# Two-layer hybrid block in fp32: normed feed-forward features made earlier, their low parts on GpSimd, paired up passes from tile 4

## The chip, the cores and the metric

The kernel runs on one core of a Trainium2 chip. The core has five engines that work side by side, each through its own queue in order: TensorE (PE, matrix products), VectorE (DVE), ScalarE (ACT), GpSimd (POOL) and SyncE (SP, which issues most of the DMAs). They wait for each other through semaphores. SBUF holds the tiles; TensorE writes its products to PSUM, which has eight banks of 128 partitions by 2 KB. The metric is the device time of one execution in microseconds, as a median over runs.

## The reference, cut to what matters

Two layers over 256 tokens of width 1024. Each layer has three branches (a gated spatial mixer, a state-space mixer, a differential attention) that are merged and projected, and then the feed forward with which the change deals:

```
x = x + merged @ w_out[layer]
h = rmsnorm(x, ffn_norm_g[layer])                        # x * rsqrt(mean(x*x) + EPS) * g
up = causal_dwconv(h @ ffn_w_up[layer], ffn_conv_w[layer], ffn_conv_b[layer])   # 3 taps along the tokens
gate, val = jnp.split(up, 2, axis=-1)                    # 2816 features each
x = x + (jax.nn.silu(gate) * val) @ ffn_w_down[layer]
```

All data are fp32.

## The kernel before, in words

**Products in two parts.** TensorE's operands are split in two: a high part (rounded to the format of the product) and a low part (what is left). A product of fp32 accuracy is then three products: high by high, high by low and low by high (`mm3`, lines 278 to 280). Weights arrive by DMA in one stream of blocks `raw` (1 MB, two halves each). For each half ScalarE makes the high part `whi` (line 231) and VectorE the low part `wlo` (line 235), both 128x1024. There are five buffers of each (`NWB`), and the program makes them four halves ahead of their use, so a new `whi` waits until TensorE is done with the half that had its buffer. The numbers in `whi49_0` are the block and its half.

**The feed forward.** The hidden features are worked through in 22 tiles j of 128 gate and 128 value features. Of each tile, "up" makes gate (m = 0) and value (m = 1) from one half of weights each. After tile 3, and then after each second tile, comes a "down" block that adds two finished tiles to the four accumulators `acc`. The order on TensorE is up 0, 1, 2, 3, down 0, up 4, 5, down 1, up 6, 7, down 2 and so on.

The up products come in two forms:

- Tiles before `MERGE` use features that are scaled by the norm's weight but not yet divided by the norm (`f_hi`, `f_lo`), since the norm of a token isn't known while they run. Each half is 24 products of 256 columns (`feat_half`). The result is multiplied by the norm's row (`fn_row`, one factor for each token) when it is taken out of PSUM, by `normed` (line 712, VectorE, tile `fu`).
- Tiles from `MERGE` on use features `hm` that are fully normed, with high and low parts beside each other. One product of 512 columns gives high by high and high by low, one of 256 columns gives low by high: 16 products a half (`feat_merged`, lines 299 to 303). Each half then takes a bank of its own, and `gather` adds its two parts: a copy on ScalarE (line 1095) and an addition on VectorE (line 1096).

**Making `hm`.** The generator `renorm` makes `hm` in four blocks b of two feature tiles each. In the kernel before: VectorE multiplies x by the norm's row (line 1072, tile `xn`, 128x512), ScalarE scales each half of it by the weight column `gcol` (line 1077, 128x256), ScalarE rounds it to the high part (line 1078), and VectorE subtracts to get the low part (line 1080). It runs as a side job: `tick` is called after each up or down half block and advances the job by its rate (0.5 here, so one step every two halves), and `finish` forces what is left before tile `MERGE`. The job starts after tile 1, once the norm's row is there.

**From tile to `act`.** For each tile, `hidden` runs the three-tap convolution on `fu`: for each m one ScalarE operation (line 756) and two VectorE operations on the tile `fy` (line 761, 128x255 and 128x254). For each second tile follow, on both tiles at once, silu on ScalarE (line 1117, the first one with a table load ahead of it), the product of gate and value on VectorE (line 1118, `fy<-fy`), and the split in `act`: high part on ScalarE (line 347), low part on VectorE (line 349). Down 0 uses the `act` of tiles 0 and 1.

**The order on the engines.** The program is written once for all engines, and a scheduler of the framework sets the order in each engine's queue from the order of writing, from priorities and from its own estimates. The queues are then fixed; on the chip each engine goes through its queue in order. Tiles of kinds `s2` (`fu`, `xn`, seven buffers) and `s4` (`hm`, `fy`, `act`, nineteen) share their slots, and a new tile waits until the last reader of its slot is done.

Of the kernel before, what the change touches and what calls it, by code (L numbers as in the profile page):

```python
# [14 lines left out]
AF = mybir.ActivationFunctionType  # L15
ALU = mybir.AluOpType
# [4 lines left out]
P = 128  # L21
D = 1024
S = 256
# [11 lines left out]
HP = 200  # L35


LAG, MERGE = 3, 7
CUM_WAIT = 6
ROW_WAIT = 2  # L40
WARM = 11
# [68 lines left out]
def ffn_order():  # L110
    order = []
    done = 0
    for j in range(NFT):
        order.append(("up", j))
        if j >= LAG and j % 2 == 1 and j < NFT - 1:
            order.append(("down", done))
            done += 1
    while done < NFT // 2:
        order.append(("down", done))
        done += 1  # L120
    return order
# [8 lines left out]
def block_kernel(ctx: ExitStack, tc: tile.TileContext, x, wstream, wdt, rows, prol, pcols, gains, gmw, consts, out):  # L130
    nc = tc.nc
# [9 lines left out]
    def ps(name):  # L141
        return pspool.tile([P, 512], F32, tag="ps", name=name)

    def s4(name, shape, dt=F32):
        return big.tile(shape, dt, tag="s4", name=name, bufs=NS4)

    def s2(name, shape, dt=F32):
        return sm.tile(shape, dt, tag="s2", name=name, bufs=NS2)
# [3 lines left out]
    x_sb = cpool.tile([P, 8, S], F32, name="x_sb")  # L152
    gcol = cpool.tile([P, L * G_N], F32, name="gcol")
# [86 lines left out]
    def next_half():  # L240

        while len(ready) <= AHEAD and stream["i"] < n_halves:
            load_half()
        return ready.popleft()
# [10 lines left out]
    def add_side(gen, rate):  # L255
        side.append([gen, rate, 0.0])
        return side[-1]
# [14 lines left out]
    def finish(e):  # L272
        while e in side:
            step(e)
# [31 lines left out]
    def feat_pair(o, h_hi, h_lo):  # L306

        halves = [next_half() for _ in range(2)]
        for k0, k1 in ((0, 6), (6, 8)):
            for m, (whi, wlo) in enumerate(halves):  # L310
                for k in range(k0, k1):
                    ks = slice(k * P, (k + 1) * P)
                    mm3(
                        o[:, m * S : (m + 1) * S], whi[:, ks], wlo[:, ks], h_hi[:, k, :], h_lo[:, k, :],
                        k + m == 0, k + m == 8,
                    )
        tick()
        tick()
# [130 lines left out]
    for l in range(L):  # L449
# [589 lines left out]
        for kh in range(2):  # L1039
            for t2 in range(4):  # L1040
                whi, wlo = next_half()
                for m in range(2):
                    t = 2 * t2 + m
# [18 lines left out]
        nff = {}  # L1062
        nf_side = add_side(norm_factors(f"fn{l}", nff, 2, 1), 1)

        def renorm():

            t = {}
            for b in range(5):
                if b < 4:
                    hm.append(s4(f"hm{l}_{b}", [P, 2, 2, S], F32R))  # L1070
                    t[b] = s2(f"xn{l}_{b}", [P, 2, S])
                    nc.vector.tensor_tensor(
                        t[b], x_sb[:, 2 * b : 2 * b + 2, :], nff["row"].unsqueeze(1).to_broadcast([P, 2, S]), op=ALU.mult
                    )
                    for m in range(2):
                        g = l * G_N + 8 + 2 * b + m
                        nc.scalar.activation(t[b][:, m, :], t[b][:, m, :], AF.Identity, scale=gcol[:, g : g + 1])
                    nc.scalar.activation(hm[b][:, :, 0, :], t[b], AF.Copy)
                if b:
                    nc.vector.tensor_tensor(  # L1080
                        hm[b - 1][:, :, 1, :], t[b - 1], hm[b - 1][:, :, 0, :].bitcast(F32), op=ALU.subtract
                    )
                yield
# [89 lines left out]
        for kind, j in ffn_order():  # L1173
            if kind == "down" and not acc:
                acc.extend(ps(f"acc{l}_{b}") for b in range(4))
            if kind == "up":
                if j == MERGE:
                    finish(hm_side)
                if j < MERGE:
                    outs[j] = [ps(f"up{l}_{j}")]  # L1180
                    if j == 0:
                        feat_pair(outs[j][0], f_hi, f_lo)
                for m in range(2):
                    if j >= MERGE:
                        outs.setdefault(j, []).append(ps(f"up{l}_{j}_{m}"))
                        feat_merged(outs[j][m], lambda k: hm[k // 2][:, k % 2, :, :])
                    elif j:
                        feat_half(outs[j][0][:, m * S : (m + 1) * S], f_hi, f_lo)
                    if m == 0 and j > 1:
                        gather(j - 1)  # L1190
                if j == 1:
                    finish(nf_side)
                    hm_side = add_side(renorm(), 0.5)
                    if l + 1 == L:
                        add_side(x_by_token(), 0.5)
                    gather(0)
                if j == NFT - 6 and l + 1 < L:
                    lc = layer_constants(l + 1)
                if j:
                    hidden(j - 1)  # L1200
                if j == NFT - 1:

                    with tc.high_priority(HP):
                        hidden(j)
            else:
                halves = [next_half() for _ in range(2)]
                if j < NFT // 2 - 1:
                    for kk in range(2):
                        for n in range(2):
                            for i in range(2):  # L1210
                                down_group(2 * j + kk, n, i, *halves[kk])
                    continue
                if l + 1 < L:
                    hT = hT_pair(f"h{l + 1}")
                dk = {}
                for n in range(2):
                    for i in range(2):
                        if l + 1 == L and n + i == 2:
                            last_group(halves)
                            continue  # L1220
                        for kk in range(2):
                            down_group(2 * j + kk, n, i, *halves[kk])
                        with tc.high_priority(HP):
                            if l + 1 < L:
                                dk[n, i] = s2(f"dk{l}_{n}_{i}", [P, 512])
                                nc.scalar.activation(dk[n, i], acc[2 * n + i], AF.Copy)
                            else:
                                xv = xk[i][:, n * 512 : (n + 1) * 512]
                                nc.vector.tensor_tensor(xv, acc[2 * n + i], xv, op=ALU.add)
                                nc.sync.dma_start(out[i, :, n * 512 : (n + 1) * 512], xv)  # L1230
                        if l + 1 < L and (n, i) == (1, 0):
                            turned_back(0, hT, dk)
                if l + 1 < L:
                    later = lambda args=(1, hT, dk), turned_back=turned_back: turned_back(*args)
# [88 lines left out]
```

## Time and profile before

| | |
|---|---|
| time before, median of 3 runs | 933.77 us (933.66 to 934.19) |
| the profiled execution, its own time | 933.71 us |
| its span, first to last instruction | 931.9 us |
| TensorE busy | 925.2 us (99%) |
| VectorE busy | 723.9 us (78%) |
| ScalarE busy | 596.2 us (64%) |
| GpSimd busy | 34.0 us (4%) |
| granted TensorE clock, mean | 0.999 of full speed |
| up tiles 0 to 3 of layer 0 | about 280 to 304 us |
| up tiles 0 to 3 of layer 1 | up to about 765 us |

How to read the rows: a row of a timeline has the start in microseconds from the span's start, the duration, the engine, the line, the operation, the tile written and the tiles read, their shapes, and xN where N operations in a row are merged; in brackets stands idle time before it and what ended it. Matmuls are pipelined, so the next one starts before the last has ended; the pace is read from start to start. The same holds on VectorE and ScalarE, where the next operation starts a tenth of a microsecond before the end of the last. A row of a list of waits has the engine that waited, the operation it waited with, what it waited for, then the total in us, the number of times and the longest. A row of a list of groups has the busy time in all and the mean duration in ns.

### The profile page before, as it was taken

To read this page: it belongs to the slowest core of one execution; us is meant where nothing else is said; L and a number is where in the kernel's file an instruction comes from. 1 tells how busy PE (TensorE), PEld (TensorE's weight loads), DVE (VectorE), ACT (ScalarE), POOL (GpSimd) and SP (SyncE) were. 2 spreads that over 40 slices of the span, in tenths; PEclk is the share of its full clock that TensorE was granted. 3 is DMA by queue.
4 is the path that set the end of the run, shared out by engine and by line. 5 is a ranking of instruction groups with operands and counts; after the bars stand their busy time and mean duration, and the time that the engine had idled before them with its cause. 6 is when DMAs were issued, how large, how long until landed. Compare 5 with 4: busy or idle time off the path is not lost.

```text
span 931.9 us, 14464 instructions
## 1 busy us (share of the span) xinstructions
PE 925.2 (99%) x5669; PEld 816.5 (88%) x5669; DVE 723.9 (78%) x1127; ACT 596.2 (64%) x928; POOL 34.0 (4%) x44
## 2 busy tenths in 40 slices
PE   9999999999999999999999999999999999999998
PEld 6899998888899988888889999888888999888887
DVE  6798668795678987877778975797947789787785
ACT  6675589764456756656667655887544577666663
POOL 1020010000000000000002000000000000000000
PEclk9999999999999999999999999999999999999999
DMA  9744574355455555555553555643555545555541
GB/s 325 279 163 178 181 271 175 136 180 183 181 181 177 185 181 185 183 207 193 181 181 136 183 181 182 225 181 135 181 181 181 181 165 195 183 181 183 191 168 45
DMA packets 28707, 171.63 MB, mean 184 GB/s; under 512 B 5184, under 2 KB 5728, under 8 KB 9184
## 3 DMA queue, kind: packets, MB, share of 16 engines
q1 hardware_dynamic: 27136, 166.35, 50.3%
q0 software_dynamic: 1216, 4.23, 1.4%
q8 instruction: 44, 0.72, 0.3%
q14 instruction: 23, 0.19, 0.1%
q10 hardware_dynamic: 288, 0.15, 0.1%
HBM read 169.63 MB, written 1.08 MB: 183 GB/s over the span
## 4 chain that ended last, share of the span: by engine, by line
PE 93%; ACT 5%; DMA 1%; DVE 1%; issue 0%; ACTq 0%; DVEq 0%
PE up L299 11%; PE up L300 5%; PE acc L278 4%; PE acc L280 4%; PE acc L279 4%; PE up L278 2%; PE up L279 2%; PE xbc L279 2%; PE xbc L280 2%; PE xbc L278 2%; PE up L280 2%; PE z L278 2%; PE wo L279 2%; PE z L280 2%; PE wo L278 2%; PE z L279 2%
## 5 line engine op out<-in xcount | busy, mean ns | idle before, releaser
L231 ACT ACTIVATE whi<-raw 128x1024 fp32r<-128x1024 f32 (+1 forms) x310 | 324.2, 1051 | 244.2 <-PE up L303 33.9
L235 DVE TENSOR_TENSOR wlo<-raw,whi 128x1024 fp32r<-128x1024 f32 (+1 forms) x310 | 375.7, 1216 | 129.0 <-ACT whi L231 128.2
L299 PE MATMUL up<-hm,whi 128*128 128x512 f32 x420 | 150.5, 397 | 0.0
L300 PE MATMUL up<-hm,wlo 128*128 128x256 f32 x420 | 117.8, 281 | 0.0
L299 PEld LDWEIGHTS up<-hm,whi 128*128 128x128 f32 x420 | 79.0, 188 | 16.9
L761 DVE SCALAR_TENSOR_TENSOR fy<-fu,pc,fy 128x255 f32<-128x255 f32 (+1 forms) x176 | 80.4, 480 | 12.3 <-ACT fy L756 10.7
L300 PEld LDWEIGHTS up<-hm,wlo 128*128 128x128 f32 x420 | 79.3, 189 | 2.5
L756 ACT ACTIVATE fy<-fu,pc 128x256 f32<-128x256 f32 x88 | 51.1, 594 | 35.9 <-DVE fu L1096 32.1
L278 PE MATMUL acc<-whi,act 128*128 128x512 f32 (+1 forms) x176 | 68.7, 390 | 0.2 <-ACT act L347 0.2
L280 PE MATMUL acc<-whi,act 128*128 128x512 f32 (+1 forms) x176 | 68.3, 389 | 0.0
L279 PE MATMUL acc<-wlo,act 128*128 128x512 f32 (+1 forms) x176 | 68.3, 388 | 0.0
L278 PE MATMUL up<-f_hi,whi 128*128 128x256 f32 x224 | 63.8, 285 | 0.0
L279 PE MATMUL up<-f_lo,whi 128*128 128x256 f32 x224 | 63.4, 283 | 0.0
L280 PE MATMUL up<-f_hi,wlo 128*128 128x256 f32 x224 | 63.4, 283 | 0.0
L278 PE MATMUL xbc<-h_hi,whi 128*128 128x256 f32 x192 | 55.3, 288 | 0.0
L280 PE MATMUL xbc<-h_hi,wlo 128*128 128x256 f32 x192 | 54.3, 283 | 0.0
L279 PE MATMUL xbc<-h_lo,whi 128*128 128x256 f32 x192 | 54.3, 283 | 0.0
L279 PEld LDWEIGHTS up<-f_lo,whi 128*128 128x128 f32 x224 | 43.0, 192 | 0.2
L278 PEld LDWEIGHTS up<-f_hi,whi 128*128 128x128 f32 x224 | 43.0, 192 | 0.2
L280 PEld LDWEIGHTS up<-f_hi,wlo 128*128 128x128 f32 x224 | 42.9, 192 | 0.0
L280 PEld LDWEIGHTS acc<-whi,act 128*128 128x128 f32 x176 | 33.0, 188 | 7.5 <-DVE act L349 0.6
L279 PEld LDWEIGHTS acc<-wlo,act 128*128 128x128 f32 x176 | 33.1, 188 | 6.8
(322 smaller groups left out, 2201.2 us busy)
## 6 DMA issues: line engine op xcount, KB each, us to landing
raw<-in_wstream SPq DMA_DIRECT2D x152, 1024.0 KB, 4.8
seg<-scr POOLq DMA_DIRECT2D x8, 512.0 KB, 6.7
rows<-in_rows SPq DMA_DIRECT2D x2, 648.0 KB, 6.9
x_sb<-in_x SPq DMA_DIRECT2D x4, 256.0 KB, 5.8
raw<-in_wstream SPq DMA_DIRECT2D x4, 256.0 KB, 5.0
raw<-in_wstream SPq DMA_DIRECT2D x2, 512.0 KB, 7.1
out_x<-xk SPq DMA_DIRECT2D x3, 256.0 KB, 2.0
gmw<-in_gmw SPq DMA_DIRECT2D x2, 256.0 KB, 7.1
```

Of the source, the lines that this page charges most:

```text
L231: split = nc.scalar.activation(hi[:, cs], src[:, cs], AF.Copy)
L235: low = nc.vector.tensor_tensor(lo[:, cs], src[:, cs], hi[:, cs].bitcast(F32), op=ALU.subtract)
L278: nc.tensor.matmul(o, a_hi, b_hi, start=start, stop=False)
L279: nc.tensor.matmul(o, a_hi, b_lo, start=False, stop=False)
L280: nc.tensor.matmul(o, a_lo, b_hi, start=False, stop=stop)
L299: nc.tensor.matmul(o, whi[:, ks], hk.rearrange("p a t -> p (a t)"), start=k == 0, stop=False)
L300: nc.tensor.matmul(o_a, a_lo, b_hi, start=False, stop=False)
L756: nc.scalar.activation(y, u, AF.Identity, bias=pcl[:, bcol : bcol + 1], scale=pcl[:, wcol + taps - 1 : wcol + taps])
L761: nc.vector.scalar_tensor_tensor(y[:, d:], u[:, : S - d], pcl[:, w : w + 1], y[:, d:], op0=ALU.mult, op1=ALU.add)
```

## The change

Three edits in one. `MERGE` goes from 7 to 4, so tiles 4, 5 and 6 take the paired passes too. The side job that makes `hm` runs at a rate of 1.5 steps a half block in place of 0.5, so it is done within 3.5 half blocks instead of 10. And its operations change: the product with the norm's row and the scaling by the weight become one VectorE operation of 128x256 for each half (`scalar_tensor_tensor`, line 1074), in place of one of 128x512 on VectorE and two of 128x256 on ScalarE; the low part is subtracted on GpSimd (line 1079) in place of VectorE. After the diff's removed line the line numbers behind it are smaller by one: in the changed kernel silu has line 1116, the product of gate and value 1117, and the copy and addition of `gather` 1094 and 1095.

```diff
--- before.py
+++ after.py
@@ -35,7 +35,7 @@
 HP = 200
 
 
-LAG, MERGE = 3, 7
+LAG, MERGE = 3, 4
 CUM_WAIT = 6
 ROW_WAIT = 2
 WARM = 11
@@ -1069,15 +1069,14 @@
                 if b < 4:
                     hm.append(s4(f"hm{l}_{b}", [P, 2, 2, S], F32R))
                     t[b] = s2(f"xn{l}_{b}", [P, 2, S])
-                    nc.vector.tensor_tensor(
-                        t[b], x_sb[:, 2 * b : 2 * b + 2, :], nff["row"].unsqueeze(1).to_broadcast([P, 2, S]), op=ALU.mult
-                    )
                     for m in range(2):
                         g = l * G_N + 8 + 2 * b + m
-                        nc.scalar.activation(t[b][:, m, :], t[b][:, m, :], AF.Identity, scale=gcol[:, g : g + 1])
+                        nc.vector.scalar_tensor_tensor(
+                            t[b][:, m, :], x_sb[:, 2 * b + m, :], gcol[:, g : g + 1], nff["row"], op0=ALU.mult, op1=ALU.mult
+                        )
                     nc.scalar.activation(hm[b][:, :, 0, :], t[b], AF.Copy)
                 if b:
-                    nc.vector.tensor_tensor(
+                    nc.gpsimd.tensor_tensor(
                         hm[b - 1][:, :, 1, :], t[b - 1], hm[b - 1][:, :, 0, :].bitcast(F32), op=ALU.subtract
                     )
                 yield
@@ -1190,7 +1189,7 @@
                         gather(j - 1)
                 if j == 1:
                     finish(nf_side)
-                    hm_side = add_side(renorm(), 0.5)
+                    hm_side = add_side(renorm(), 1.5)
                     if l + 1 == L:
                         add_side(x_by_token(), 0.5)
                     gather(0)
```

What this does to the queues. First VectorE in layer 0, from the first xn operation to the product of gate and value for tiles 0 and 1 (`fy<-fy`, with which `act0_0` begins). Before:

```order
L1072 TENSOR_TENSOR xn0_0_3075<-x_sb_75,fn0_row_2999 128x512
L761 SCALAR_TENSOR_TENSOR fy0_0_3005<-fu0_0_3003,pc0_241,fy0_0_3005 128x255 x2
L761 SCALAR_TENSOR_TENSOR fy0_0_3005<-fu0_0_3003,pc0_241,fy0_0_3005 128x254 x2
L235 TENSOR_TENSOR wlo48_1_3047<-raw48_3014,whi48_1_3046 128x1024
L761 SCALAR_TENSOR_TENSOR fy0_0_3005<-fu0_1_3044,pc0_241,fy0_0_3005 128x255
L712 TENSOR_TENSOR fu0_2_3121<-up0_2_3013,fn0_row_2999 128x512
L761 SCALAR_TENSOR_TENSOR fy0_0_3005<-fu0_1_3044,pc0_241,fy0_0_3005 128x254
L761 SCALAR_TENSOR_TENSOR fy0_0_3005<-fu0_1_3044,pc0_241,fy0_0_3005 128x255
L235 TENSOR_TENSOR wlo49_0_3094<-raw49_3091,whi49_0_3093 128x1024
L761 SCALAR_TENSOR_TENSOR fy0_0_3005<-fu0_1_3044,pc0_241,fy0_0_3005 128x254
L1072 TENSOR_TENSOR xn0_1_3152<-x_sb_75,fn0_row_2999 128x512
L1118 TENSOR_TENSOR fy0_0_3005<-fy0_0_3005 128x512
```

In the changed kernel, the last twelve rows up to the same product; ahead of them, behind `fu0_0`, stand both halves of `xn0_0`, one row of `fy`, `fu0_1` and one more row of `fy`:

```order
L761 SCALAR_TENSOR_TENSOR fy0_0_3005<-fu0_0_3003,pc0_241,fy0_0_3005 128x255
L1074 SCALAR_TENSOR_TENSOR xn0_1_3080<-x_sb_75,gcol_76,fn0_row_2999 128x256
L761 SCALAR_TENSOR_TENSOR fy0_0_3005<-fu0_0_3003,pc0_241,fy0_0_3005 128x254
L235 TENSOR_TENSOR wlo48_1_3052<-raw48_3014,whi48_1_3051 128x1024
L1074 SCALAR_TENSOR_TENSOR xn0_1_3080<-x_sb_75,gcol_76,fn0_row_2999 128x256
L1074 SCALAR_TENSOR_TENSOR xn0_2_3086<-x_sb_75,gcol_76,fn0_row_2999 128x256 x2
L761 SCALAR_TENSOR_TENSOR fy0_0_3005<-fu0_1_3049,pc0_241,fy0_0_3005 128x255 x2
L761 SCALAR_TENSOR_TENSOR fy0_0_3005<-fu0_1_3049,pc0_241,fy0_0_3005 128x254 x2
L235 TENSOR_TENSOR wlo49_0_3105<-raw49_3102,whi49_0_3104 128x1024
L1074 SCALAR_TENSOR_TENSOR xn0_3_3133<-x_sb_75,gcol_76,fn0_row_2999 128x256 x2
L712 TENSOR_TENSOR fu0_2_3138<-up0_2_3013,fn0_row_2999 128x512
L1117 TENSOR_TENSOR fy0_0_3005<-fy0_0_3005 128x512
```

All four blocks of xn now stand ahead of the product, as eight operations of 128x256, where two of 128x512 stood; fu, fy and wlo are the same in number. In layer 1 the order is the same, and one hm low part that stood ahead of the product is gone from VectorE.

ScalarE in layer 0, around silu (`fy<-fy`) and the high part of `act0_0`, which opens down 0. Before:

```order
L231 ACTIVATE whi49_0_3093<-raw49_3091 128x1024
L1117 ACT_TABLE_LOAD
L1117 ACTIVATE fy0_0_3005<-fy0_0_3005 128x512
L231 ACTIVATE whi49_1_3123<-raw49_3091 128x1024
L1077 ACTIVATE xn0_1_3152<-xn0_1_3152,gcol_76 128x256
L347 ACTIVATE act0_0_3006<-fy0_0_3005 128x512
L1077 ACTIVATE xn0_1_3152<-xn0_1_3152,gcol_76 128x256
L231 ACTIVATE whi50_0_3172<-raw50_3170 128x1024
L1078 ACTIVATE hm0_1_3151<-xn0_1_3152 128x2x256
```

In the changed kernel:

```order
L231 ACTIVATE whi49_0_3104<-raw49_3102 128x1024
L1077 ACTIVATE hm0_1_3079<-xn0_1_3080 128x2x256
L1077 ACTIVATE hm0_2_3085<-xn0_2_3086 128x2x256
L231 ACTIVATE whi49_1_3140<-raw49_3102 128x1024
L1116 ACT_TABLE_LOAD
L1116 ACTIVATE fy0_0_3005<-fy0_0_3005 128x512
L231 ACTIVATE whi50_0_3183<-raw50_3181 128x1024
L347 ACTIVATE act0_0_3006<-fy0_0_3005 128x512
L1077 ACTIVATE hm0_3_3132<-xn0_3_3133 128x2x256
```

The two scalings around act are gone; the high parts of hm blocks 1 and 2 and the weight half `whi49_1` moved ahead of the table load and silu, and the weight half `whi50_0` ahead of act. In layer 1 the weight halves `whi126_1` and `whi127_0` stand between silu and act, behind the copies of x by token and the table load.

GpSimd between the norm of the feed forward in layer 0 and the norm that opens layer 1, where `fn0_rp` is the inverse root of the norm. Before:

```order
L341 TENSOR_SCALAR fn0_r_2964<-fn0_s_2962 128x2
L343 TENSOR_TENSOR fn0_rp_2966<-fn0_r_2964,mhalf_79 128x2
L341 TENSOR_SCALAR an1_r_4846<-an1_s_4844 128x2
L343 TENSOR_TENSOR an1_rp_4848<-an1_r_4846,mhalf_79 128x2
L341 TENSOR_SCALAR rqk1_5139<-ssq1_5003 128x32
```

In the changed kernel:

```order
L343 TENSOR_TENSOR fn0_rp_2966<-fn0_r_2964,mhalf_79 128x2
L1079 TENSOR_TENSOR hm0_0_3044<-xn0_0_3045,hm0_0_3044 128x2x256
L1079 TENSOR_TENSOR hm0_1_3079<-xn0_1_3080,hm0_1_3079 128x2x256
L1079 TENSOR_TENSOR hm0_2_3085<-xn0_2_3086,hm0_2_3085 128x2x256
L1079 TENSOR_TENSOR hm0_3_3132<-xn0_3_3133,hm0_3_3132 128x2x256
L341 TENSOR_SCALAR an1_r_4806<-an1_s_4804 128x2
```

The four low parts stand there in a row; nothing else of GpSimd's lies within the feed forward. TensorE's order is the same in both kernels, with 16 in place of 24 products a half in tiles 4 to 6.

## The prediction

> **What bounds the kernel now.** I read the page's head first, then the list of what TensorE waited for, then the timelines of the first feed-forward stretch of each layer, engine by engine.
>
> ```profile
> span 931.9 us, 14464 instructions
> PE 925.2 (99%) x5669; PEld 816.5 (88%) x5669; DVE 723.9 (78%) x1127; ACT 596.2 (64%) x928; POOL 34.0 (4%) x44
> ```
>
> TensorE (PE) is busy in 99% of the span, so a microsecond counts only if it changes how long TensorE takes or how long it waits. GpSimd (POOL) has nearly nothing to do.
>
> ```profile
> PE warm L174 <- DVE cold L171: 1.2, 1, 1.2
> ...
> PE acc L278 <- ACT act L347: 0.2, 1, 0.2
> ```
>
> The first and the last of five rows. The last is the one wait of TensorE in the feed forward, and it lies where the change works: the first "down" product of layer 0 waits for `act`, the hidden values of tiles 0 and 1.
>
> ```profile
> 303.93 0.28 PE L280 MATMUL up<-f_hi,wlo 128*128 128x256 f32 x1
> 304.37 0.50 PE L278 MATMUL acc<-whi,act 128*128 128x512 f32 x1 [0.16 <-ACT act L347]
> ...
> 326.92 0.28 PE L278 MATMUL up<-f_hi,whi 128*128 128x256 f32 x1
> ...
> 332.67 0.40 PE L299 MATMUL up<-hm,whi 128*128 128x512 f32 x1
> ...
> 338.29 0.39 PE L278 MATMUL acc<-whi,act 128*128 128x512 f32 x1
> ...
> 764.87 0.28 PE L280 MATMUL up<-f_hi,wlo 128*128 128x256 f32 x1
> ...
> 765.78 0.48 PE L278 MATMUL acc<-whi,act 128*128 128x512 f32 x1
> ```
>
> TensorE's timeline (start, duration, then the operation). Tile 3 ends and down 0 begins at 304.37 in layer 0 and, behind the transposes of x, at 765.78 in layer 1. The three rows between show tile 6 in three passes (326.92 to 332.67, 5.75 us) and tile 7 in paired passes (332.67 to 338.29, 5.62 us). So down 0 has no slack: in layer 0 `act` is already last. What comes before it on VectorE (DVE) and ScalarE (ACT):
>
> ```profile
> 294.46 1.28 DVE L712 TENSOR_TENSOR fu<-up,fn_row 128x512 f32<-128x512 f32 x2
> 295.66 0.68 DVE L1072 TENSOR_TENSOR xn<-x_sb,fn_row 128x512 f32<-128x512 f32 x1
> 296.26 1.66 DVE L761 SCALAR_TENSOR_TENSOR fy<-fu,pc,fy 128x255 f32<-128x255 f32 x4
> 297.84 1.22 DVE L235 TENSOR_TENSOR wlo<-raw,whi 128x1024 fp32r<-128x1024 f32 x1
> 298.98 0.48 DVE L761 SCALAR_TENSOR_TENSOR fy<-fu,pc,fy 128x255 f32<-128x255 f32 x1
> ...
> 302.89 0.69 DVE L1118 TENSOR_TENSOR fy<-fy 128x512 f32<-128x512 f32 x1
> ...
> 754.54 1.28 DVE L712 TENSOR_TENSOR fu<-up,fn_row 128x512 f32<-128x512 f32 x2
> ...
> 762.97 0.68 DVE L1080 TENSOR_TENSOR hm<-xn,hm 128x512 fp32r<-128x512 f32 x1
> 763.57 0.68 DVE L1118 TENSOR_TENSOR fy<-fy 128x512 f32<-128x512 f32 x1
> ```
>
> ```profile
> 300.52 1.28 ACT L1117 ACT_TABLE_LOAD   x1
> 301.82 0.63 ACT L1117 ACTIVATE fy<-fy 128x512 f32<-128x512 f32 x1
> 302.36 1.05 ACT L231 ACTIVATE whi<-raw 128x1024 fp32r<-128x1024 f32 x1
> 303.30 0.49 ACT L1077 ACTIVATE xn<-xn,gcol 128x256 f32<-128x256 f32 x1
> 303.70 0.61 ACT L347 ACTIVATE act<-fy 128x512 fp32r<-128x512 f32 x1
> ```
>
> Read from start to start, VectorE pays 0.60 us for a 128x512 operation (294.46 to 295.66 for two), 0.395 for a 128x256 one with a column (296.26 to 297.84 for four) and 1.14 for a low part of weights (297.84 to 298.98). With these paces the order of before can be added up: from 294.46 to the product `fy<-fy` stand three fu, two xn, eight fy and two wlo, 1.80 + 1.20 + 3.16 + 2.28 = 8.44 us, which gives 302.90; the trace has 302.89. In layer 1 one hm low part more (0.60) gives 754.54 + 9.04 = 763.58; the trace has 763.57. VectorE runs without a gap there, so this queue can be walked for the new order.
>
> **The change, part by part.**
>
> Paired passes on tiles 4 to 6: per tile 5.75 - 5.62 = 0.13 us less of TensorE, six tiles in the two layers, 0.8 us; I take 0.7, since the last of before's tiles may carry an edge. Each such tile is emptied by two ScalarE copies and two VectorE adds in place of one VectorE product. That is after down 0, where VectorE loses more (the old xn and hm work) than it gains, beside products that hold TensorE 5.6 us a tile: nothing.
>
> ```profile
> L1095 ACT ACTIVATE fu<-up 128x256 f32<-128x256 f32 x60 | 21.9, 366 | 2.6 <-PE up L303 2.6
> L1077 ACT ACTIVATE xn<-xn,gcol 128x256 f32<-128x256 f32 x16 | 7.4, 497 | 0.8 <-DVE xn L1072 0.8
> L377 DVE SCALAR_TENSOR_TENSOR f_lo<-x_sb,gcol,f_hi 128x256 fp32r<-128x256 f32 x16 | 7.0, 480 | 0.0
> ```
>
> Groups (busy in total, mean ns of one, idle before). ScalarE loses sixteen scalings of 497 ns and gains 24 copies of 366 ns, off the path. The new xn operation has the shape and operands of L377, 480 ns, 0.395 from start to start.
>
> The earlier making: this is the term that decides. Ahead of the product of tiles 0 and 1, VectorE now has all eight xn operations of 128x256 instead of two of 128x512; fu, fy and wlo there are the same in number. That is 8 x 0.395 = 3.16 in place of 1.20: the product starts at 294.46 + 10.40 = 304.86 and ends (0.69) at 305.55. ScalarE then makes act (0.62, with 0.05 on either side for the hand-over): 306.2, and down 0 starts at 306.27 instead of 304.37, 1.9 us of wait. In layer 1 the low part that stood ahead is gone: the product ends at 754.54 + 10.40 + 0.69 = 765.63, but ScalarE has a weight half in front of act whose buffer comes free only with tile 3's last product (764.87 + 0.28); 765.2 + 0.95 + 0.62 and its own queue before that give 766.8, and down 0 starts at 766.9 instead of 765.8, 1.1 us. Behind the waiting product stand all later ones on TensorE; nothing on its queue passes.
>
> Low parts on GpSimd: eight operations of 128x512 that the trace shows on GpSimd only as a product.
>
> ```profile
> 20.71 1.09 POOL L341 TENSOR_SCALAR an_r<-an_s 128x2 f32<-128x2 f32 x1 [19.58 <-DVE an_s L403]
> ...
> 23.43 1.31 POOL L433 TENSOR_TENSOR gmw<-gmw,cst 128x512 f32<-128x512 f32 x1
> ...
> 50.70 5.53 POOL L343 TENSOR_TENSOR rqk0p<-rqk,mhalf 128x32 f32<-128x32 f32 x1
> ...
> 150.56 1.74 POOL L433 TENSOR_TENSOR gmw<-gmw,cst 128x512 f32<-128x512 f32 x1 [27.45 <-DMA gmw<-in_gmw]
> ...
> 289.57 0.20 POOL L341 TENSOR_SCALAR fn_r<-fn_s 128x2 f32<-128x2 f32 x1 [73.72 <-DVE fn_s L403]
> ```
>
> ```profile
> 20.54 2.35 DVE L235 TENSOR_TENSOR wlo<-raw,whi 128x1024 fp32r<-128x1024 f32 x2
> ...
> 50.07 2.45 DVE L761 SCALAR_TENSOR_TENSOR cv<-cu,pc,cv 128x255 f32<-128x255 f32 x6
> ...
> 150.44 0.69 DVE L349 TENSOR_TENSOR yalo<-gmy,yahi 128x512 fp32r<-128x512 f32 x1
> ...
> 152.16 1.22 DVE L871 TENSOR_TENSOR seg<-seg,cbm 128x1024 f32<-128x1024 f32 x1
> ```
>
> 1.31 us with VectorE idle, 1.74 when it started 0.12 us into a VectorE operation that reads two tiles of SBUF: the 0.43 more is just what was left of that operation (150.44 + 0.60 - 150.56 = 0.48). A row of two elements took 1.09 beside a wlo and 0.20 alone, though that was also its first use. So GpSimd seems to wait until VectorE's two-tile operation has read. What VectorE pays in return no row shows: six fy kept 0.395 beside the 5.5 us power, whose tiles are 32 wide, and seg at 152.16 was on time. Bounds: 0 and 1.31 us for each low part (a gain is excluded; the removed work is counted above). I take 1.1, nearest to the 128x512 rows: 1.31 less the 0.20 that an operation of two elements takes, and not above the 152.16 - 151.04 = 1.12 in which GpSimd had no two-tile operation beside it. Three low parts are asked for before the product (from about 296.9, 300.8 and 302.1, at the ends of their high parts), and VectorE there has nearly only two-tile operations: 3.3 us on the product. Layer 0: 1.9 + 3.3 = 5.2. Layer 1: 1.1 + 3.3, less 0.55 that ScalarE's queue had already cost (765.68 against 766.21): 3.9.
>
> [...]
>
> The waits added: fu of tile 3 waits for the first low part (its slot was xn's), with VectorE's later wlo behind it; the first use in tile 4 waits for each. The fourth low part is ready by about 308 to 312, tile 4 starts 5.6 us after down 0, so neither waits. No DMA is added or moved, and SP's queue is the same.
>
> Sum: 933.71 (the profiled execution; 0.06 below the median of 933.77) + 5.2 + 3.9 - 0.7 = 942.1 us, 0.9% slower. About 0.2%, 1.9 us, is what a measurement can tell from no change.
>
> **The rivals.**
>
> No blocking: VectorE keeps its pace beside GpSimd, as the six fy did. 933.7 + 1.9 + 1.1 - 0.7 = 936.0.
>
> Blocking for the whole instruction: 1.31 per low part, 5.8 + 4.5 - 0.7 = +9.6, 943.3; with 1.74 each nearer 946. Against it are the same fy. [...]
>
> Not slower, to be measured: ScalarE's queue alone sets act. If VectorE, unblocked, reaches the product by 304.25 rather than 304.86 (xn at 0.32 instead of 0.395 would do), the order weight split, table load, silu on ScalarE still ends silu near 304.2, and act comes 1.3 us late in layer 0 and 1.0 in layer 1: 933.7 + 2.3 - 0.7 = 935.3, within 0.2%. Against it: the walk met before within 0.01 us.
>
> Hidden altogether: act on time, 933.0. It needs the product 2 us earlier than the walk has it.
>
> [...]
>
> **How the numbers follow.** Forecast 0.45; no blocking 0.25; whole instruction 0.10; ScalarE alone 0.10; hidden 0.03; starved 0.04; something else 0.03. The range, 935.3 to 944.0, holds the forecast, no blocking, half of ScalarE alone and of whole instruction: about 0.8. Slower: forecast, whole instruction, starved and 0.21 of no blocking (its 2.3 us are close to the bound), 0.80; same 0.18; faster 0.02, since no case gains more than 0.8 us.
>
> **What would show it.** TensorE's waits should name act at down 0 in both layers, 5.2 and 3.9 us, or 1.9 and 1.1 without blocking. VectorE rows beside L1079 should last longer or start late by about 1.1 us per low part; if their means stay at 480 and 1220 ns, the blocking is wrong. Paired tiles 4 to 6 should take 5.62 us. A product `fy<-fy` before 304.3 would make the walk wrong, and waits of TensorE at tile 4 the deadline.

## The result, and the profile after

| | before | after |
|---|---|---|
| median | 933.76 us (933.66 to 934.19, 4 runs) | 946.50 us (944.60 to 947.84, 4 runs) |
| ratio | | 1.0136, 95% interval 1.0123 to 1.0148 |
| granted TensorE clock in these runs | 0.999 | 0.993, 0.993, 0.996, 0.993 |

The change makes the kernel 12.7 us (1.4%) slower. The forecast was 942.1 us with a range up to 944.0: the direction was right, the size 4.4 us too small. The page's head after, from the profiled execution (947.21 us, span 945.4 us, 13.5 us longer than before's):

```profile
span 945.4 us, 14310 instructions
PE 929.9 (98%) x5573; PEld 815.7 (86%) x5573; DVE 729.4 (77%) x1133; ACT 593.1 (63%) x924; POOL 48.2 (5%) x52
```

TensorE (PE) has fewer instructions than before (5573 against 5669, the paired passes), yet is busy 4.7 us longer. So the time is not all waiting: some products must have become slower. The list of TensorE's waits comes first. In before it named `act` at down 0 with 0.2 us:

```profile
PE acc L278 <- ACT act L347: 8.8, 2, 5.1
```

Two waits, 8.8 us in all: 5.14 us in layer 0 and 3.65 in layer 1, at the place and for the tile that the prediction named. TensorE's timeline of layer 0, from the last product of tile 3 on:

```profile
303.94 0.28 PE L280 MATMUL up<-f_hi,wlo 128*128 128x256 f32 x1
309.36 0.79 PE L278 MATMUL acc<-whi,act 128*128 128x512 f32 x1 [5.14 <-ACT act L347]
309.96 0.63 PE L279 MATMUL acc<-wlo,act 128*128 128x512 f32 x1
310.38 0.63 PE L278 MATMUL acc<-whi,act 128*128 128x512 f32 x1
...
314.65 0.63 PE L278 MATMUL acc<-whi,act 128*128 128x512 f32 x1
315.07 0.48 PE L279 MATMUL acc<-wlo,act 128*128 128x512 f32 x1
315.39 0.40 PE L280 MATMUL acc<-whi,act 128*128 128x512 f32 x1
315.62 0.40 PE L278 MATMUL acc<-whi,act 128*128 128x512 f32 x1
...
317.68 0.39 PE L299 MATMUL up<-hm,whi 128*128 128x512 f32 x1
```

This is what the prediction did not have. After the wait, the products of down 0 start 0.425 us apart (309.96 to 310.38), until about 315.2; from there on they start 0.23 apart, as in before. Fourteen products take 6.03 us (309.36 to 315.39) where 14 x 0.228 = 3.19 would do: 2.8 us. The view by stretches of time shows why. Its columns are the stretch, its length, the busy time of PE, PEld, DVE, ACT and POOL, then the granted clock (1.00 is full speed), the DMA share and GB/s:

```profile
304.00:308.40 4.40, 0.22 (x2) 0.02 (x1) 4.40 (x7) 2.86 (x3) 0.85 (x1) 1.00 0.15 63
308.40:315.20 6.80, 5.84 (x14) 4.58 (x15) 6.32 (x9) 2.45 (x5) 2.75 (x1) 0.50 0.45 154
315.20:320.00 4.80, 4.80 (x25) 4.06 (x24) 3.44 (x5) 3.31 (x5) 0.00 (x0) 1.00 0.33 106
771.00:776.00 5.00, 2.42 (x21) 2.19 (x20) 5.00 (x8) 3.30 (x4) 1.33 (x1) 1.00 0.27 113
776.00:782.90 6.90, 5.83 (x14) 4.58 (x15) 6.00 (x10) 4.38 (x9) 2.52 (x1) 0.51 0.43 153
```

The granted clock falls to one half at about 308.4 us, while TensorE is still waiting, and comes back at about 315.2; in layer 1 the same from 776.0 to 782.9. TensorE's last product had ended 4.2 us before the fall in layer 0 (at 304.22) and 2.6 us before it in layer 1 (at 773.43, with the transposes of x). Layer 1 loses 2.8 us in the same way. The sum of the profiled execution is then: longer waits 5.14 - 0.16 + 3.65 = 8.6, slow products 2 x 2.8 = 5.6, paired passes -0.7: 13.5 us, which is what the span shows. Taken over the whole of down 0, from its first product to the first of tile 4, the slow products come to 5.3 us (8.32 and 8.27 in place of 5.57 and 5.69), and the sum to 13.3.

Why `act` is late, on VectorE (DVE) and GpSimd (POOL):

```profile
296.26 0.69 DVE L712 TENSOR_TENSOR fu<-up,fn_row 128x512 f32<-128x512 f32 x1
296.86 1.91 DVE L761 SCALAR_TENSOR_TENSOR fy<-fu,pc,fy 128x254 f32<-128x254 f32 x2
...
301.80 3.72 DVE L761 SCALAR_TENSOR_TENSOR fy<-fu,pc,fy 128x255 f32<-128x255 f32 x4
...
307.97 0.68 DVE L1117 TENSOR_TENSOR fy<-fy 128x512 f32<-128x512 f32 x1
```

```profile
296.89 1.59 POOL L1079 TENSOR_TENSOR hm<-xn,hm 128x512 fp32r<-128x512 f32 x1 [6.34 <-ACT hm L1077]
301.83 3.02 POOL L1079 TENSOR_TENSOR hm<-xn,hm 128x512 fp32r<-128x512 f32 x2 [3.35 <-ACT hm L1077]
```

Two `fy` take 1.91 us in place of 0.87, beside one low part on GpSimd; four take 3.72 in place of 1.66, beside two. That is 1.03 us of VectorE for each low part. The second of the first two `fy`, by itself:

```profile
297.25 1.51 DVE L761 SCALAR_TENSOR_TENSOR fy<-fu,pc,fy 128x255 f32<-128x255 f32 x1
```

It starts while GpSimd's low part runs (296.89 to 298.48) and ends at 298.76, 0.28 us after it. The product of tiles 0 and 1 comes at 307.97 (302.89 in before).

### The profile page after: what moved, and what is told of

Read it like the earlier page. It is cut to its first block, busy times and chain, and to the rows that moved or that the text cites. A ratio compares the mean times of both kernels' runs of the same rounds, so it can differ in the third digit from the quotient of the medians.

```text
span 945.4 us, 14310 instructions
## 1 busy us (share of the span) xinstructions
PE 929.9 (98%) x5573; PEld 815.7 (86%) x5573; DVE 729.4 (77%) x1133; ACT 593.1 (63%) x924; POOL 48.2 (5%) x52
## 4 chain that ended last, share of the span: by engine, by line
PE 90%; ACT 5%; DVE 3%; DMA 1%; issue 1%; ACTq 0%; DVEq 0%
PE up L299 12%; PE up L300 6%; PE acc L278 4%; PE acc L280 4%; PE acc L279 4%; PE xbc L279 2%; PE xbc L278 2%; PE xbc L280 2%; PE up L303 2%; PE z L278 2%; PE wo L279 2%; PE z L280 2%; PE z L279 2%; PE wo L280 2%; PE wo L278 2%; ACT whi L231 2%
## 5 line engine op out<-in xcount | busy, mean ns | idle before, releaser
L299 PE MATMUL up<-hm,whi 128*128 128x512 f32 x504 | 180.7, 398 | 0.0
L300 PE MATMUL up<-hm,wlo 128*128 128x256 f32 x504 | 141.5, 281 | 0.0
L299 PEld LDWEIGHTS up<-hm,whi 128*128 128x128 f32 x504 | 94.9, 188 | 20.3
L300 PEld LDWEIGHTS up<-hm,wlo 128*128 128x128 f32 x504 | 95.3, 189 | 3.0
L278 PEld LDWEIGHTS acc<-whi,act 128*128 128x128 f32 x176 | 34.4, 195 | 15.6 <-ACT act L347 9.2
L280 PEld LDWEIGHTS acc<-whi,act 128*128 128x128 f32 x176 | 34.3, 195 | 7.8 <-DVE act L349 0.4
L279 PEld LDWEIGHTS xbc<-h_lo,whi 128*128 128x128 f32 x192 | 36.9, 192 | 0.1
L278 PEld LDWEIGHTS xbc<-h_hi,whi 128*128 128x128 f32 x192 | 36.8, 192 | 0.1
L278 PE MATMUL z<-h_hi,whi 128*128 128x256 f32 x128 | 36.9, 288 | 0.0
L280 PEld LDWEIGHTS xbc<-h_hi,wlo 128*128 128x128 f32 x192 | 36.8, 192 | 0.0
L278 PE MATMUL up<-f_hi,whi 128*128 128x256 f32 x128 | 36.6, 286 | 0.0
```

Source lines behind the costliest of these rows:

```text
L278: nc.tensor.matmul(o, a_hi, b_hi, start=start, stop=False)
L279: nc.tensor.matmul(o, a_hi, b_lo, start=False, stop=False)
L280: nc.tensor.matmul(o, a_lo, b_hi, start=False, stop=stop)
L299: nc.tensor.matmul(o, whi[:, ks], hk.rearrange("p a t -> p (a t)"), start=k == 0, stop=False)
L300: nc.tensor.matmul(o_a, a_lo, b_hi, start=False, stop=False)
```

## The experiments

Times are medians; the kernel before ran beside them on the same chip, at 933.4 to 933.7 us.

| kernel | median, us | ratio to before, 95% | waits for act's high part, layer 0 and 1, in its profile | granted clock, profiled run |
|---|---|---|---|---|
| after | 946.50 | 1.0136 (1.0123 to 1.0148) | 5.14, 3.65 | 0.993 |
| e1 low part written only | 936.64 | 1.0038 (1.0024 to 1.0053) | 2.04, 0.93 | 0.999 |
| e2 low part on VectorE | 937.34 | 1.0043 (1.0028 to 1.0057) | 2.64, 1.53 | 0.999 |
| e4 old operations, new pace | 936.40 | 1.0031 (1.0019 to 1.0043) | 2.22, 0.66 | 0.999 |
| e3 TensorE kept busy, 16 and 8 | 946.49 | 1.0136 (1.0121 to 1.0151) | 1.67, 1.92 | 0.998 |
| e7 TensorE kept busy, 25 and 20 | 943.77 | 1.0107 (1.0092 to 1.0122) | none | 1.000 |
| e9 idle alone, no GpSimd | 944.34 | 1.0116 (1.0101 to 1.0131) | 4.82, 3.08 | 0.996 |
| e10 low part with one read | 939.97 | 1.0071 (1.0054 to 1.0088) | 3.16, 1.42 | 0.998 |
| e5 new operations, old pace | 935.12 | 1.0016 (1.0007 to 1.0025) | 0.18, 0 | 0.999 |
| e6 fused operation alone | 933.21 | 0.9994 (0.9985 to 1.0002) | 0, 0 | 1.000 |
| e8 paired from tile 6 | 933.51 | 0.9995 (0.9987 to 1.0004) | 0, 0 | 0.999 |

**What do GpSimd's low parts cost?** Two kernels take GpSimd's reading away. e1 writes zeros in place of the low part, which is thus left out:

```diff
-                    nc.gpsimd.tensor_tensor(
-                        hm[b - 1][:, :, 1, :], t[b - 1], hm[b - 1][:, :, 0, :].bitcast(F32), op=ALU.subtract
-                    )
+                    nc.gpsimd.memset(hm[b - 1][:, :, 1, :].bitcast(F32), 0.0)
```

> GpSimd writes zeros into the low parts instead of subtracting (the low part of the normed features is left out), so it reads no SBUF; VectorE's, ScalarE's and TensorE's queues stay row for row. Theory (VectorE is blocked while a GpSimd operation reads SBUF, and a TensorE that has idled for over 3 us works at half clock for some 6 us): the four fy beside L1079 take 1.67 us again instead of 3.72, down 0 waits 1.9 us in layer 0 and 1.1 in layer 1, the clock stays at 1.0, 936.0 us. Rival 1 (any GpSimd operation of that size blocks, or VectorE's own order is what is slow): 945 to 948. Rival 2 (the 4.6 us beyond the waits come from the paired tiles 4 to 6 or from late weights, not from the clock): 940 to 941.

TensorE's timeline, GpSimd's and VectorE's in e1:

```profile
306.45 0.50 PE L278 MATMUL acc<-whi,act 128*128 128x512 f32 x1 [2.04 <-ACT act L347]
...
768.71 0.50 PE L278 MATMUL acc<-whi,act 128*128 128x512 f32 x1 [0.93 <-ACT act L347]
```

```profile
290.70 1.92 POOL L1079 MEMSET hm<- 128x512 f32 x4
```

```profile
297.06 0.87 DVE L761 SCALAR_TENSOR_TENSOR fy<-fu,pc,fy 128x254 f32<-128x254 f32 x2
...
300.95 1.66 DVE L761 SCALAR_TENSOR_TENSOR fy<-fu,pc,fy 128x255 f32<-128x255 f32 x4
```

The time, 936.64 us, is 0.6 above the 936.0 expected. The waits of 2.04 and 0.93 us are the prediction's order term, 1.9 and 1.1. The `fy` are at their old pace. The 3 and 6 us of the theory stand for what after shows, waits of 5.14 and 3.65 us and slow products from 309.36 to 315.2, 5.9 us. In e1 the clock stayed at 1.00 from 304 to 309 us. But the zeros were written at 290.7 us, since nothing made them wait for the high part; so e1 shows the stretch without GpSimd, and not what writing alone would cost beside VectorE.

e2 does the subtraction on VectorE again (`nc.vector.tensor_tensor` on the same line):

> The change with its low parts on VectorE again. Theory: two low parts of 0.60 us stand ahead of the product of tiles 0 and 1, where fu of tile 2 has moved behind it, so the product starts at 294.46 + 11.0 = 305.5 in layer 0: down 0 waits about 2.5 us there and about 1.7 in layer 1, too short for the clock to fall; 937.3 us. Rival 1 (VectorE was not blocked by GpSimd, its queue is just full): more work on it, so no faster than 946. Rival 2 (the extra beyond the waits does not come from the clock): about 942.

It came as expected: waits of 2.64 and 1.53 us, and a clock of 0.999 in the profiled execution. So in this stretch a low part is dearer on GpSimd, where it takes 1.03 us from VectorE, than on VectorE itself, at 0.60.

e10 sends GpSimd to the same place with one tile to read in place of two; the low part is left out (zero):

```diff
-                    nc.gpsimd.tensor_tensor(
-                        hm[b - 1][:, :, 1, :], t[b - 1], hm[b - 1][:, :, 0, :].bitcast(F32), op=ALU.subtract
-                    )
+                    nc.gpsimd.tensor_scalar(
+                        hm[b - 1][:, :, 1, :], hm[b - 1][:, :, 0, :].bitcast(F32), 0.0, None, op0=ALU.mult
+                    )
```

> The changed kernel, with GpSimd's subtraction replaced by a multiplication of the high part with zero: one tile is read in place of two, at the same place and behind the same wait (the low part is left out). Theory (what GpSimd reads or writes in SBUF holds VectorE's two-tile operations up for most of GpSimd's own time): the three fy rows beside it last longer than 0.40 us each by 0.4 to 0.9 us per GpSimd operation, TensorE waits 3.2 to 4.7 us in layer 0: 939 to 944 us. Rival (only an operation with two tiles read on GpSimd holds VectorE up): the fy keep 0.40 us, waits of 2.0 and 0.9 us as with the low part written only: 936.6 us.

GpSimd and VectorE in e10:

```profile
296.45 1.80 POOL L1079 TENSOR_SCALAR hm<-hm 128x512 fp32r<-128x512 f32 x1 [6.34 <-ACT hm L1077]
300.71 3.33 POOL L1079 TENSOR_SCALAR hm<-hm 128x512 fp32r<-128x512 f32 x2 [2.46 <-ACT hm L1077]
```

```profile
296.42 1.22 DVE L761 SCALAR_TENSOR_TENSOR fy<-fu,pc,fy 128x254 f32<-128x254 f32 x2
...
300.68 2.01 DVE L761 SCALAR_TENSOR_TENSOR fy<-fu,pc,fy 128x255 f32<-128x255 f32 x4
302.61 1.63 DVE L235 TENSOR_TENSOR wlo<-raw,whi 128x1024 fp32r<-128x1024 f32 x1
```

The rival (only an operation with two tiles read) falls: VectorE loses 0.35 us beside the first (1.22 against 0.87), 0.35 and 0.41 beside the next two. That is below the 0.4 to 0.9 expected, and far below the 1.7 us that each takes on GpSimd. With a second tile to read, in after, the price is 1.03 in place of about 0.37 us, although GpSimd's own time gets no longer. The two operations differ in kind as well (a subtraction, and a multiplication by a constant), so that the second tile alone makes the difference is not shown. The four runs also show the clock's part: 938.51 us at a granted clock of 1.000, 939.39 at 0.998, 940.54 and 941.01 at 0.996, with the same instructions.

**Is it the new operations or their place?** e4 has the new pace and MERGE 4 with the operations of before; e5 the reverse.

> The change's pace and pairing (rate 1.5, paired passes from tile 4) with the operations of before: product with the row on VectorE, two scalings on ScalarE, low part on VectorE. Theory: ahead of the product stand two fu, four xn and two low parts of 0.60, eight fy and two wlo, 10.2 us from 294.46: product at 304.7, down 0 waits about 2 us in layer 0 and 1 to 1.5 in layer 1, clock at 1.0: 936 to 937. So the earlier making alone would cost 2 to 3 us whatever the operations, and the operations on GpSimd the other ten. Rival (the earlier making does not delay act by itself): 933.

e4 came as expected. Its runs at a clock of 0.999 or 1.000 took 935.71 to 935.79 us, 2.0 above before, and 2.22 - 0.16 + 0.66 - 0.7 = 2.0; those at 0.998 took 937.0 to 937.6.

```diff
-LAG, MERGE = 3, 4
+LAG, MERGE = 3, 7
...
-                    hm_side = add_side(renorm(), 1.5)
+                    hm_side = add_side(renorm(), 0.5)
```

> The changed kernel's operations (weight and row in one VectorE operation, low parts on GpSimd) with the pace and the start of paired passes of before (0.5 steps a half block, MERGE 7). Theory (GpSimd's low part holds VectorE up by about 1.03 us, and only what stands ahead of the product of tiles 0 and 1 counts): ahead of that product stand two new xn (2 x 0.395) in place of two old ones (2 x 0.60) and one low part on GpSimd: -0.41 + 1.03 = +0.62, so TensorE waits about 0.8 us at down 0 of layer 0 in place of 0.16; in layer 1 one old low part of 0.60 also falls away, so nothing changes there: 934.4 us (933.9 to 935.5), and the clock stays at 0.999 or 1.000, since no wait reaches 3 us. Rival (no blocking outside the crowded stretch, or blocking only when two low parts run back to back): the product comes 0.41 earlier, no wait, 933.5. Rival (the operations alone make the kernel slow, whatever the pace): near 941 or more.

935.12 us, in the range given, but not by the way that was expected. GpSimd's first low part and VectorE beside it in layer 0 of e5:

```profile
299.72 3.04 POOL L1079 TENSOR_TENSOR hm<-xn,hm 128x512 fp32r<-128x512 f32 x1 [9.54 <-ACT hm L1077]
```

```profile
300.39 1.22 DVE L235 TENSOR_TENSOR wlo<-raw,whi 128x1024 fp32r<-128x1024 f32 x1
301.52 0.68 DVE L712 TENSOR_TENSOR fu<-up,fn_row 128x512 f32<-128x512 f32 x1
302.12 1.19 DVE L1117 TENSOR_TENSOR fy<-fy 128x512 f32<-128x512 f32 x1
```

Here the low part lasted 3.04 us, and VectorE's `fy` and `wlo` beside it kept their pace; only the product behind `fu` took 0.5 us more, not the 1.03 expected. The low part ended at 302.76, inside that product; why there, no run shows. TensorE waited 0.18 us at down 0 of layer 0 in place of the 0.8 expected. The cost came in layer 1, where none was expected: the second low part ran beside VectorE's low part of `act`, which took 1.77 us in place of 0.68, and down 0 waited for that:

```profile
765.13 1.42 POOL L1079 TENSOR_TENSOR hm<-xn,hm 128x512 fp32r<-128x512 f32 x1 [2.15 <-ACT hm L1077]
```

```profile
765.32 1.77 DVE L349 TENSOR_TENSOR act<-fy,act 128x512 fp32r<-128x512 f32 x1
```

```profile
767.15 0.50 PE L280 MATMUL acc<-whi,act 128*128 128x512 f32 x1 [0.86 <-DVE act L349]
```

This wait of 0.86 us is most of the 1.15 by which e5's profiled execution (934.86) lies above that of before (933.71); that the time fell in the range given was luck. So the price was not the same beside different operations of VectorE: 1.03 us beside the `fy` of after, 0.5 and 1.1 here. The clock was 0.999 or 1.000 in all eleven runs of e5, as expected. The limit of 3 us given for that is an estimate, between e2's wait of 2.64 us at 0.999 and after's of 3.65 with a fall; e3, below, has a fall behind waits of 1.92 and 1.02 us. The same operations that cost 12.7 us at the new pace cost 1.4 at the old one.

e6 keeps the fused operation alone, with `nc.vector` for the low part and pace and MERGE of before:

> Before's pace and MERGE 7, low parts on VectorE as before; only the product with weight and row is one VectorE operation of 128x256 for each half. Theory: ahead of the product of tiles 0 and 1 stand 0.79 in place of 1.20 us, so the wait of 0.16 us at down 0 of layer 0 goes and nothing comes: 933.6 us (933.4 to 933.9). Rival (VectorE has 3.16 in place of 2.40 us of xn in each layer, and that is late for the weights' low parts around tiles 4 to 6): 934.2 or more, with waits of TensorE for wlo or hm.

933.21 us is 0.5 less than before and just under the range given, and the interval of the ratio takes in 1: no difference that this measurement settles.

**Does idleness halve the clock?** Between tile 3 and down 0, e3 and e7 give TensorE products of zeros into a bank of their own; all else is as in after.

```diff
             if kind == "down" and not acc:
+                busy = ps(f"busy{l}")
+                for _ in range(16 - 8 * l):
+                    nc.tensor.matmul(busy, cold[:, 0:P], cold, start=True, stop=True)
+            if kind == "down" and not acc:
                 acc.extend(ps(f"acc{l}_{b}") for b in range(4))
```

> The change, with products of zeros that nothing waits for put on TensorE between tile 3 and down 0: 16 of 512 columns in layer 0 (about 3.5 us), 8 in layer 1 (1.7 us). Theory (the idle TensorE loses its clock): act comes at the same time as in the change, TensorE idles only about 1.7 and 1.9 us ahead of down 0, its products there run at 0.228 us from start to start instead of 0.425, granted clock 0.999; 5.3 us less, with up to 0.6 for the low part of act, which is now needed earlier in the row: 941 to 942. Rival (the slow down 0 has another cause, such as its operands or DMA traffic): 946 to 948, products still 0.425 apart.

The time missed what was expected: 946.49 us, no better than after. The profiled run took 945.0 at a clock of 0.998, the others 946.3 to 947.3 at 0.996. TensorE's timeline of e3 in both layers says why:

```profile
303.75 3.63 PE L1176 MATMUL busy<-cold 128*128 128x512 bf16 x15
309.04 0.50 PE L278 MATMUL acc<-whi,act 128*128 128x512 f32 x1 [1.67 <-ACT act L347]
309.38 0.40 PE L279 MATMUL acc<-wlo,act 128*128 128x512 f32 x1
...
774.61 0.50 PE L278 MATMUL acc<-whi,act 128*128 128x512 f32 x1 [1.92 <-ACT act L347]
774.95 0.40 PE L279 MATMUL acc<-wlo,act 128*128 128x512 f32 x1
775.19 0.39 PE L278 MATMUL acc<-whi,act 128*128 128x512 f32 x1
776.59 0.65 PE L280 MATMUL acc<-whi,act 128*128 128x512 f32 x1 [1.02 <-DVE act L349]
777.04 0.63 PE L279 MATMUL acc<-wlo,act 128*128 128x512 f32 x1
```

In layer 0 the products of down 0 now run at full pace. In layer 1 the clock still fell (0.63 on the mean from 776 to 779 us), in a stretch with waits of 1.92 and 1.02 us and less than a microsecond of work between them. Eight useless products were too few, and the test said little about the total. e7 repeats it with `range(25 - 5 * l)`:

> The changed kernel with products of zeros on TensorE between tile 3 and down 0, 25 in layer 0 and 20 in layer 1, which cover the whole wait for act (16 and 8 in the kernel before, where the profile shows the granted clock fall in layer 1 alone and 1.9 and 1.0 us of wait left in both). They change nothing that is computed. Theory (the idle time, not the low parts, halves the clock): down 0 runs at 0.23 us a product in both layers, granted clock 0.999 or 1.000, and although TensorE works through some 10 us of useless products, the time is 942.8 us (942.0 to 943.6), 3 to 4 us less than the changed kernel. Rival (the slow products of down 0 come from something else, such as operands that VectorE and GpSimd still work on): 946.5 as with the changed kernel, products 0.425 us apart.

```profile
303.60 5.57 PE L1176 MATMUL busy<-cold 128*128 128x512 bf16 x25
308.91 0.50 PE L278 MATMUL acc<-whi,act 128*128 128x512 f32 x1
309.25 0.40 PE L279 MATMUL acc<-wlo,act 128*128 128x512 f32 x1
309.99 0.51 PE L280 MATMUL acc<-whi,act 128*128 128x512 f32 x1 [0.34 <-DVE act L349]
...
776.52 0.50 PE L280 MATMUL acc<-whi,act 128*128 128x512 f32 x1 [0.86 <-DVE act L349]
776.86 0.39 PE L278 MATMUL acc<-whi,act 128*128 128x512 f32 x1
```

Full pace in both layers, clock 1.000, and 943.77 us: 2.7 less than after, although TensorE does some 10 us of useless work. Its four runs lie within 0.44 us, those of after within 3.2. It is 1.0 above the 942.8 expected and 0.2 above the range given; the waits of 0.34 and 0.86 us for act's low part, which this order of products meets and that of after does not, are about that much.

e9 makes the counterpart, idle time without GpSimd: before, with three operations more on VectorE ahead of the product.

```diff
+            for _ in range(3 if j == 1 else 0):
+                nc.vector.tensor_tensor(y[:, 1, js, :], y[:, 1, js, :], y[:, 1, js, :], op=ALU.max)
             nc.vector.tensor_tensor(y[:, 1, js, :], y[:, 0, js, :], y[:, 1, js, :], op=ALU.mult)
```

> The kernel before, with three extra VectorE operations of 128x512 ahead of the product of tiles 0 and 1 (each takes the larger of a tile and the tile itself, so nothing changes in what is computed); nothing is moved to GpSimd. With them, two low parts of weights that stood behind the product in layer 0 now stand ahead of it, so the product comes 3 x 0.60 + 2 x 1.14 + 0.60 = 4.7 us later in layer 0 and about 4.1 us in layer 1, and TensorE waits about 4.9 and 3.9 us, nearly what it waits in the changed kernel (5.1 and 3.65). Theory (idle time of TensorE alone halves the clock and costs 2 to 2.7 us more per layer): 933.74 + 4.7 + 3.9 + about 4.5 = 946.8 us (944.5 to 948.5, spread over 2 us or more between runs), granted clock 0.993 to 0.997, products of down 0 0.425 us apart. Rival (the slow products need GpSimd beside them): 942.3, up to 943.5 with a wait for act's low part, and a clock of 0.999 or 1.000.

```profile
309.34 0.79 PE L278 MATMUL acc<-whi,act 128*128 128x512 f32 x1 [4.82 <-ACT act L347]
309.94 0.63 PE L279 MATMUL acc<-wlo,act 128*128 128x512 f32 x1
...
776.70 0.50 PE L278 MATMUL acc<-whi,act 128*128 128x512 f32 x1 [3.08 <-ACT act L347]
777.04 0.40 PE L279 MATMUL acc<-wlo,act 128*128 128x512 f32 x1
```

In layer 0, after 4.82 us of waiting, down 0 starts at the slow pace (0.50 of full speed from 308 to 314 us) with nothing on GpSimd: the rival falls. In layer 1 the wait was 3.08 us where 3.9 was expected, the clock did not fall (1.00 from 773 to 780 us), and so the time, 944.34, lies just under the range given. All four runs had a clock of 0.996. The numbers fit one fall: half speed for 6.8 us is 3.4 us of lost clock, and 3.4 / 942.7 = 0.0036.

**A version to beat both.** e8 is e6 with `MERGE` 6 and a pace of 0.65:

> A version meant to beat both: weight and row in one VectorE operation, low parts on VectorE, paired passes from tile 6, pace 0.65 in place of 0.5, so that still only two xn stand ahead of the product of tiles 0 and 1. Theory: the wait of 0.16 us goes, and tile 6 of both layers gains 0.13 us each: 933.77 - 0.16 - 0.26 = 933.35 us (933.1 to 933.6). Rival (VectorE, busy all the time from 298 to 327 us in the kernel before, can't bring the last low part one tile earlier, or brings weights' low parts late): TensorE waits for hm or wlo at tiles 4 to 6, 933.8 to 935.

933.51 us, in the range given, 0.2 below before and 0.3 above e6; neither difference is settled. What the paired passes can give here lies below what this measurement can tell.

## Why the prediction was right and where it was wrong

**The order term was right.** 1.9 and 1.1 us forecast; 2.04 and 0.93 in e1, where only the order is left. The rival in which ScalarE alone sets `act` falls with it, as does the hidden change. The 0.04 given to a starved GpSimd found nothing in the trace: its first three low parts had ended by 304.85.

**The term for GpSimd was right in kind and nearly in size.** 1.1 us of VectorE for each of three low parts ahead of the product; 1.03 by the `fy` rows, and the waits of after less those of e1 are 3.1 and 2.7 us (3.3, less 0.55 in layer 1, forecast). Waits: 5.2 and 3.9 forecast, 5.14 and 3.65 measured. That the 0.20 taken off 1.31 is why it is 1.03 is not shown. The rival of blocking for the whole instruction, 1.31 or more, misses these rows by 0.28; its time "nearer 946" was met by another cause. A block of VectorE until GpSimd's operation has finished nearly fits after, where the `fy` shown above ended 0.28 us behind GpSimd's low part, and does not fit e10, where the `fy` beside GpSimd's 1.80 us lost 0.35 and ended at 297.64, 0.6 us before GpSimd did.

**The paired passes** met -0.7: tiles 4 to 7 take 5.64 us each after, and by TensorE's rows the tiles 4 to 6 of both layers are 0.66 us shorter in all. No wait of TensorE at tile 4 stands in the list.

**The step that failed is the sum itself**, "5.2 + 3.9 - 0.7". It charged a wait at its own length, and took the products behind it as if nothing had happened to them. Each wait cost 2.8 us more, since the clock fell during it and stayed at one half for 6.8 us: 5.6 us in the profiled execution. The delay of down 0 itself was 0.5 us less than forecast (5.14 - 0.16 + 3.65 = 8.6 in place of 9.1). Together 942.1 + 5.6 - 0.5 = 947.2, and this execution took 947.21. Before's own rows hardly showed it: its longest wait of TensorE behind the start was 0.5 us and its clock 0.999. Only at the very end of its trace does the clock fall to one half (at 930.56, 2.6 us after TensorE's last product had ended at 927.98), where nothing is left to slow down. That the clock could fall in the forecast waits of 5.2 and 3.9 us as well was not weighed. In after it fell 4.2 us after the last product in layer 0 and 2.6 us after it in layer 1.

**The spread between runs has the same cause in part, by inference.** The kernel's instructions are the same in each run; the clock differs. Runs of after with 0.993 took 945.8 to 947.8, the one with 0.996 took 944.6. Two half-speed stretches of 6.8 us lose 6.8 us of full clock, and 6.8 / 945.4 = 0.0072, which is 0.993; one such stretch gives 0.996. The 2.0 us between the runs at 0.993 are not explained by this: a stretch that lies more in the wait and less on the products would cost less at the same mean clock, but only the profiled run's falls were seen.

## What to carry to other kernels

A wait of TensorE can cost more than its length: here the waits of 5.14 and 3.65 us, in each of which the clock halved for 6.8 us, cost another 2.8 us each behind them, and useless products that filled the wait bought 2.7 us back. Work given to an idle engine is free only if the busy engine keeps its pace beside it: a subtraction of 0.60 us on VectorE took 1.03 us of VectorE's time when GpSimd did it. And before work is pulled earlier, add up the queue up to the nearest deadline: the changed operations cost 12.7 us at the pace that pulls them all ahead of it, where the old ones cost 2.7 (e4), and 1.4 us at the old pace, mostly behind it.

## What the runs showed of the hardware

**When the clock falls.** In waits of 5.14 us (after, layer 0), 4.82 (e9, layer 0), 3.65 (after, layer 1) and 3.16 (e10, layer 0) it fell 4.2, 3.3, 2.6 and 3.0 us after TensorE's last product had ended. In layer 1 of e3 it fell at 776.8, 0.2 us behind a wait of 1.02 us, with 1.0 us of products and a wait of 1.92 us before that. It stayed at 1.00 across a wait of 3.08 us in layer 1 of e9 and one of 2.04 in layer 0 of e1. So the length of the wait alone does not sort these cases, and what does, no run was made to test.

**How long it stays down.** 3.41 us in e3 and e10, where TensorE idled no more than 0.13 us behind the fall; 6.82 in both layers of after and about 6.8 in e9, where it idled another 0.95 to 1.5 us. Whether this idle time is the cause is not shown.

**Shorter waits.** In e1, e2 and e4, with longest waits of 2.0 to 2.6 us in their profiled runs, the executions at a clock of 0.997 or 0.998 took 1.2 to 2.5 us more than those at 0.999 or 1.000. As an estimate from the stretches above, one of 3.41 us at half speed loses 1.7 us of clock, which is 0.002 of 935 us. So the clock seems to have fallen there too, but no trace caught it.

**GpSimd beside VectorE.** A GpSimd operation of 128x512 that reads SBUF took 1.4 (e5, layer 1) to 3.0 us (e5, layer 0) beside VectorE. VectorE's loss went from 0.35 us (e10) to 1.1 (e5, layer 1). It differed between the two operations of GpSimd, 0.37 us for e10's multiplication and 1.03 for after's subtraction, and between operations of VectorE, 0.5 and 1.1 us in e5. What sets it stays open.
